# First part in a fixed order, its biases added later, and half of a layer's rows written by an adding DMA

## The chip, the cores and the metric

The kernel runs on one core of a Trainium2 chip. The metric is the time of one execution on the device in microseconds (us). Three executions of the kernel before took 2216.36, 2218.04 and 2220.47 us.

## The reference

A batch of one, 512 latent rows and 256 context rows of width 1024, passes two blocks of two layers each, all in fp32. The change lies in the first block:

```
for i in range(DEPTH):                                  # 2 layers
    sh1, sc1, g1, sh2, sc2, g2 = adaln(c, w_mod[i], b_mod[i])        # silu(c) @ w_mod + b_mod
    a_lat = modulate(x, norm1_g[i], sh1, sc1)           # rmsnorm(x, g) * (1 + sc) + sh
    # layer 0: pool mixer for x and ctx; layer 1: attention over ctx and x
    x = x + g1 * y_lat
    x = x + g2 * hier_moe(modulate(x, norm2_g[i], sh2, sc2), ...)
    # layer 0 does the same for the 256 context rows, with its own shift and scale

pool_mixer: four windows (2, 4, 8, 16), one to each 256 channels:
    y = (window mean of h - h) @ w_pool[g] + b_pool ;  return y * ls
hier_moe:  16 experts in 4 groups: the best group by g_logits, the best two experts in it,
    hid = silu(h @ w_gate) * (h @ w_up) * gates ;  sum of hid @ w_down
```

The second block (stick-breaking attention, dilated attention, two convolutional feed-forward parts) follows, and but for one small sum in the dilated attention it is left as it was.

## The kernel before

One program builds instructions for five engines: TensorE (PE), VectorE (DVE), ScalarE (ACT), GpSimd (POOL) and SyncE (SP). Each runs its own list in order; a scheduler sets the lists, mostly from the order in which the Python code emits the work and from when operands are expected. SP issues the weight loads (`load_raw`, L314) in pieces of 128 x 1024 fp32, 512 KB each, into 6 small buffers and a `ring` of larger ones; a load waits until its buffer is free and until its DMA semaphore, one of eight that all queues of SP and ACT share, has come free.

**First part (0 to 137 us).** x and ctx lie transposed, channels on partitions, in 8 chunks (`NCH`). The modulation is computed in blocks of 512 columns: `adaln_mm` (L380) multiplies by 16 matmuls and copies the result (L385, ACT); `adaln_end` transposes it (L177) and reduces it on DVE (L393). `pool_pre` makes normalized and shifted rows (L479, L481), `pool_win` runs a window over them (L495, L507), `pool_back` first adds the bias of the pool to x (L518, ACT), multiplies by the window's weight (L521) and adds the product to x (L523, DVE). `moe_chunk` scales a chunk (L587) and squares it (L589) on ACT and feeds both to the router's logits in a group of four matmuls (L594). `moe_close` evacuates the logits of one segment (L622), transposes and reduces them (L627), makes the reciprocal root mean square (`rstd_from`, whose root is L192) and leaves in `st.trs` one pair of functions to each block of 128 rows; `moe_tr` transposes such a block, and DVE writes it with scale and shift (L648) for a DMA to `h2d` in device memory (L649).

**The experts.** `moe_run` computes the routing on DVE (L685 to L780) with counting matmuls on PE between (L716 to L722, L775); the last result is the list of row indices per expert (L778). GpSimd gathers each expert's rows from h2d by index (L834); PE transposes them (L177), ACT and DVE split them in two fp32r parts (L854, L855), and weights are split likewise: ACT rounds `hi` (L294), DVE subtracts for `lo` (L295). Gate and up take three matmuls to each product (L353 to L355), down the same; ACT evacuates down's result (L898) and sends it off (L899). Layer 0 takes 768 rows with room for 128 per expert, layer 1 takes 512 with room for 96. `Stream.side("a")` and `side("b")` run two adaLN blocks of layer 1 just before layer 0's experts, and each of their halves lets one item more of the weights go (`st.more(1)`).

In the trace, tiles of 128 x 2048 are named s, tiles of 128 x 516 t, small ones sm, g and tv.

Of the kernel before, what the change touches and what calls it, by code (L numbers as in the profile page):

```python
# [25 lines left out]
D = 1024  # L26
NCH = 8
# [36 lines left out]
def build(tc, A, out, stop=None, dbg=None):  # L64
# [98 lines left out]
    def vc(name, i=0, n=1):  # L163
        o = _VEC[name] + i
        return vec[:, o : o + n]

# [155 lines left out]
    class Stream:  # L322
# [50 lines left out]
    def adaln_mm(l, nb, st=None, got=None):  # L373
# [3 lines left out]
        for u in range(2):  # L377
# [4 lines left out]
            if st:  # L382
                st.more(1)
# [128 lines left out]
    def pool_back(r, g):  # L512
        xr, n, _ = rows[r]
        ps_p = pooled.pop((r, g))
        g_, b_ = gl[r, g // 2]
        for f in range(2):
            c = 2 * g + f
            S.activation(xr[:, c, :], xr[:, c, :], AF.Identity, bias=b_[:, c % 4 : c % 4 + 1])  # L518
# [4 lines left out]
            V.scalar_tensor_tensor(xr[:, c, :], ps[:, :n], g_[:, c % 4 : c % 4 + 1], xr[:, c, :], op0=ALU.mult, op1=ALU.add)  # L523
# [29 lines left out]
    def moe_start(l, segs, cap):  # L553
# [5 lines left out]
        for xr, n, r in segs:  # L559
            q = K()  # L560
            q.xr, q.n, q.r, q.nb, q.tb0, q.psl, q.seen, q.due = xr, n, r, n // 128, st.ntb, None, 0, []
# [17 lines left out]
    def moe_chunk(st, i, c):  # L579
# [3 lines left out]
        if q.psl is None:  # L583
            q.psl = PS()
            q.hts = [s8() for _ in range(NCH * q.n // 2048)]
            q.a2 = gain_mod(st.l, "norm2_g", 4, q.r, f"a2_{q.r}")
        S.activation(hch(q, c), q.xr[:, c, :], AF.Copy, scale=q.a2[:, c : c + 1])  # L587
        sq = t2()
        S.activation(sq[:, : q.n], q.xr[:, c, :], AF.Square)  # L589
# [8 lines left out]
    def moe_shift(st, i):  # L598
# [11 lines left out]
        q.b2r = half("b2")  # L610
        for h_ in range(2):
            pt = PS()
            for c in range(4):
                transpose(pt[:, c * 128 : c * 128 + 128], b2[:, 4 * h_ + c : 4 * h_ + c + 1].to_broadcast([128, 128]))
            S.copy(q.b2r[:, 512 * h_ : 512 * h_ + 512], pt)

    def moe_close(st, i):
# [4 lines left out]
        S.copy(ev[:, :n], q.psl[:, :n])  # L622
# [5 lines left out]
        q.rs = rstd_from(lg[:, :, 20], 1.0 / D, [128, nb], f"n2_{q.r}")  # L628
        lg = lg[:, :, 0:20]
# [3 lines left out]
        def tr(b):  # L633
# [10 lines left out]
            def second():  # L644
                ht = half("ht")
                for h_, pt in enumerate(pts):
                    hs_ = slice(512 * h_, 512 * h_ + 512)
                    V.scalar_tensor_tensor(ht[:, hs_], pt, q.rs[:, b : b + 1], q.b2r[:, hs_], op0=ALU.mult, op1=ALU.add)  # L648
                (G if len(st.segs) > 1 else S).dma_start(st.h2d[(q.tb0 + b) * 128 : (q.tb0 + b) * 128 + 128, :], ht)  # L649
# [3 lines left out]
        st.trs += [tr(b) for b in range(nb)]  # L653

# [13 lines left out]
    def moe_run(st, wst):  # L668
# [121 lines left out]

        def late():


            gd = gsm([128, N, 4], tag="gd")
            V.tensor_tensor(gd, gl_, bc(gm.rearrange("p (n o) -> p n o", o=1), [128, N, 4]), op=ALU.subtract)
# [4 lines left out]
            v1, v2 = (gsm([128, N], tag=f"v{j}") for j in range(2))  # L800
            for v_, va in ((v1, v1a), (v2, v2a)):
                V.tensor_tensor(va, va, goh, op=ALU.mult)
                V.reduce_sum(v_, va, axis=AX.X)
            ed = gsm([128, N], tag="ed")
            V.tensor_tensor(ed, v2, v1, op=ALU.subtract)
# [34 lines left out]
        def gather(e):  # L840
            xg[e] = half("xg")
            gather_rows(xg[e][0:cap, :], idx[0:cap, e : e + 1])
# [16 lines left out]
        def gate_up(e):  # L859
# [10 lines left out]
            S.activation(sg[0:cap, 0:256], pg[0:cap, 0:256], AF.Silu)  # L870
            V.tensor_tensor(sg[0:cap, 256:512], sg[0:cap, 0:256], pg[0:cap, 256:512], op=ALU.mult)
            pgs[e] = sg

# [80 lines left out]
        for e in range(3):  # L954
            gather(e)
        wst.side("c")
        if not wgu:
            with tc.issue_after(gated.ins):
                moe_weights(st, wst, 0, V)
        rows_t(0)  # L960
        for e in range(NEXP + 1):
# [17 lines left out]
            if e == NEXP - 1:  # L979
                onehots(segs[0])  # L980
            if e < NEXP:
# [101 lines left out]


    mst = moe_start(0, rows, 128)
    sss = [stats(0)]
    adaln_block(0, 0)
    rb[0] = bcast(sss[0].compact("n1_0"), T)
    adaln_block(0, 2)
# [1429 lines left out]
```

## Time and profile before

| | |
|---|---|
| median of three executions | 2218.04 us (2216.36 to 2220.47) |
| the profiled execution | 2218.79 us, its span 2217.0 us |
| mean granted TensorE clock | 0.973 |
| PE, DVE, ACT, POOL busy | 93%, 64%, 50%, 23% of the span |

A busy share is the sum of an engine's instruction times over the span. The places of the change lie in the first 305 us and, for layer 1, in 600 to 706 us. A row of the timeline gives the start, the time, the engine and the line of neighbouring instructions of one form (xN of them), and in brackets how long the engine stood idle ahead of it and what released it.

### The profile page before, as it was taken

Reading aid. Unit: us, or ns where it says so; the run is one execution under the profiler, and the core shown is the slowest. Engines: PE = TensorE matmul, PEld = TensorE weight load, DVE = VectorE, ACT = ScalarE, POOL = GpSimd, SP = SyncE. Lnnn points to the kernel's source line nnn. Section 1 sums busy time; section 2 is a strip of 40 time slices with the busy share of each in tenths; the row PEclk is TensorE's granted clock in tenths of the full one; section 3 lists DMA queues with packets and bytes.
Section 4 is the critical chain, followed back from the end, with each engine's and each line's share of the span. In section 5 each row is a group of like instructions: output and inputs, shape, how many; then the busy total and the mean of one; then the engine's idle time right before and its main releaser. Section 6 shows DMA issues by size and latency. Waiting matters only on the chain.

```text
span 2217.0 us, 32294 instructions
## 1 busy us (share of the span) xinstructions
PE 2067.5 (93%) x12233; PEld 1683.7 (76%) x12233; DVE 1418.8 (64%) x2304; ACT 1102.1 (50%) x1967; POOL 509.6 (23%) x513
## 2 busy tenths in 40 slices
PE   6869998999994999999999999999999999999997
PEld 1348767788863767776698888999878888888997
DVE  4579878778726987367847666626363568565633
ACT  3648864488833886344434434324253455343422
POOL 1011021477201212245423101014100024101011
PEclk9889999999997999999999999999999999999998
DMA  9699973124606996321113333332322212333321
GB/s 376 260 351 398 417 282 101 50 77 137 217 21 219 369 391 211 99 77 48 58 52 102 94 100 91 98 93 68 97 86 86 67 48 89 101 96 96 96 77 39
DMA packets 94207, 323.43 MB, mean 146 GB/s; under 512 B 11537, under 2 KB 17184, under 8 KB 93536
## 3 DMA queue, kind: packets, MB, share of 16 engines
q1 hardware_dynamic: 76480, 274.76, 36.0%
q0 software_dynamic: 7968, 28.32, 3.6%
q10 hardware_dynamic: 9600, 18.26, 2.2%
q8 instruction: 97, 1.59, 0.3%
q14 instruction: 62, 0.51, 0.1%
HBM read 301.02 MB, written 20.27 MB: 145 GB/s over the span
## 4 chain that ended last, share of the span: by engine, by line
PE 65%; DVE 7%; DMA 4%; POOL 3%; ACT 3%; issue 3%; ACTq 0%; DVEq 0%; POOLq 0%; SPq 0%
PE ps L353 19%; PE ps L355 18%; PE ps L354 18%; PE ps L177 3%; DMA s<-in_mgu_dram 1%; PE ps L1722 1%; DVE lo L295 1%; POOL raw L1762 1%; PE ps L2103 1%; PE ps L2254 1%; DVE s L1939 1%; ACT hi L294 1%; DMA raw<-in_mdn_dram 1%; PE ps L2059 1%; DVE s L1931 1%
## 5 line engine op out<-in xcount | busy, mean ns | idle before, releaser
L353 PE MATMUL ps<-s,hi 128*128 128x512 f32 (+1 forms) x1440 | 513.5, 358 | 4.3 <-DVE s L1931 3.2
L354 PE MATMUL ps<-s,hi 128*128 128x512 f32 (+1 forms) x1440 | 505.6, 351 | 3.0 <-DVE s L1939 1.8
L355 PE MATMUL ps<-s,lo 128*128 128x512 f32 (+1 forms) x1440 | 507.4, 353 | 0.0
L294 ACT CAST hi<-raw 128x1024 fp32r<-128x1024 f32 x284 | 294.0, 1047 | 419.2 <-PE ps L354 334.2
L295 DVE TENSOR_TENSOR lo<-raw,hi 128x1024 fp32r<-128x1024 f32 x232 | 288.2, 1256 | 277.5 <-ACT hi L294 277.3
L295 POOL TENSOR_TENSOR lo<-raw,hi 128x1024 fp32r<-128x1024 f32 x52 | 125.4, 2411 | 892.1 <-ACT hi L294 892.1
L353 PEld LDWEIGHTS ps<-s,hi 128*128 128x128 f32 x1440 | 270.5, 188 | 45.7 <-issue 8.0
L354 PEld LDWEIGHTS ps<-s,hi 128*128 128x128 f32 x1440 | 271.3, 188 | 41.4 <-DVE s L1939 2.4
L355 PEld LDWEIGHTS ps<-s,lo 128*128 128x128 f32 x1440 | 271.1, 188 | 41.1 <-issue 0.5
L353 PE MATMUL ps<-hi,s 128*128 128x512 f32 (+1 forms) x528 | 216.8, 412 | 4.6 <-ACT hi L294 2.0
L354 PE MATMUL ps<-lo,s 128*128 128x512 f32 (+1 forms) x528 | 211.9, 401 | 2.6 <-DVE lo L295 2.6
L355 PE MATMUL ps<-hi,s 128*128 128x512 f32 (+1 forms) x528 | 211.3, 401 | 2.5 <-DVE s L1839 2.5
L355 PE MATMUL ps<-t2r,lo 128*128 128x256 f32 (+1 forms) x640 | 188.2, 294 | 0.0
L354 PE MATMUL ps<-t2r,hi 128*128 128x256 f32 (+1 forms) x640 | 187.8, 293 | 0.0
L353 PE MATMUL ps<-t2r,hi 128*128 128x256 f32 (+1 forms) x640 | 187.8, 293 | 0.0
L353 PEld LDWEIGHTS ps<-hi,s 128*128 128x128 f32 (+1 forms) x528 | 105.3, 199 | 30.1 <-ACT hi L294 4.4
L355 PEld LDWEIGHTS ps<-hi,s 128*128 128x128 f32 (+1 forms) x528 | 105.2, 199 | 29.0 <-DVE s L1839 4.1
L354 PEld LDWEIGHTS ps<-lo,s 128*128 128x128 f32 (+1 forms) x528 | 105.9, 201 | 25.7 <-DVE lo L295 3.1
L353 PEld LDWEIGHTS ps<-t2r,hi 128*128 128x128 f32 x640 | 121.2, 189 | 5.2 <-issue 2.5
L354 PEld LDWEIGHTS ps<-t2r,hi 128*128 128x128 f32 x640 | 121.1, 189 | 5.3 <-issue 2.5
L355 PEld LDWEIGHTS ps<-t2r,lo 128*128 128x128 f32 x640 | 120.8, 189 | 5.2 <-issue 2.5
L295 DVE TENSOR_TENSOR lo<-s,hi 128x1024 fp32r<-128x1024 f32 x98 | 114.8, 1217 | 5.2 <-ACT hi L294 4.7
(371 smaller groups left out, 3667.2 us busy)
## 6 DMA issues: line engine op xcount, KB each, us to landing
raw<-in_up_dram SPq DMA_DIRECT2D x88, 512.0 KB
s<-in_mgu_dram SPq DMA_DIRECT2D x64, 512.0 KB
raw<-in_mgu_dram SPq DMA_DIRECT2D x44, 512.0 KB
raw<-in_down_dram SPq DMA_DIRECT2D x44, 512.0 KB
raw<-in_dilqkv_dram SPq DMA_DIRECT2D x36, 512.0 KB
s<-in_mdn_dram SPq DMA_DIRECT2D x34, 512.0 KB
raw<-in_wmodT_dram SPq DMA_DIRECT2D x32, 512.0 KB
s<-in_wmod_dram SPq DMA_DIRECT2D x30, 512.0 KB
```

The lines of the kernel that those rows point to most:

```text
L177: return PE.transpose(dst, src, ident if idt is None else idt)
L294: S.copy(hi, raw)
L295: eng.tensor_tensor(lo, raw, hi, op=ALU.subtract)
L353: mm(ps, ahi, bhi, start=start, stop=False)
L354: mm(ps, ahi, blo, start=False, stop=False)
L355: return mm(ps, alo, bhi, start=False, stop=stop)
L1722: mm(po_[c][o : o + 64, qb * 128 : qb * 128 + 128], vview[:, kc, c // 2 * 64 : c // 2 * 64 + 64], PTs[h_][:, kc * 128 : kc * 128 + 128], s ...
L1762: G.tensor_tensor(w, w, crow, op=ALU.mult)
L1931: V.tensor_tensor(mv, mv, bc(self.rb[:, None, 0:256], [128, 2, 256]), op=ALU.mult)
L1939: V.scalar_tensor_tensor(self.h.lo(c)[:, ts], x[:, c, ts], g_, self.h.hi(c)[:, ts], op0=ALU.mult, op1=ALU.subtract)
L2059: mm(pz[:, o : o + n], qq, kk, start=True, stop=True)
L2103: mm(po[64 * hh : 64 * hh + 64, kb * 128 : 512], vt, at[:, o : o + n], start=(kb == 0), stop=(kb == 3), tile_position=(0, 64 * hh))
```

## The change

1. `in_order()` ties each instruction of DVE, ACT and PE in the first part to the one emitted before it on its engine. The first part is written anew: blocks of adaLN come in the order 0, 2, 1, 3, 4, 8, 5, 9, 6, 7, then 10 and 11 behind the fixed part, each loaded four blocks ahead; `pool_back` is split in `back_mm` and `back_add`; chunks of x go to the logits two by two as soon as they are done. The sums of squares of ctx go over ACT and PE (`sum_stats`).
2. The pool's bias is not added there. `moe_chunk` adds it inside its two activations, and x and ctx get it in the loop of layer 0's experts, one chunk of each in expert 4 to 11 (`back_bias`, called as `side`).
3. In layer 0 the first gather is issued ahead of nine small operations of `late` (now `late_first`); `side("a")` and `side("b")` let no weights go; the four items (eight loads) that they let go before are issued behind the first gather, and the first of them waits until it has landed.
4. In layer 1 the shift rows are made early and written to h2d for row blocks 0 and 1. Later ACT evacuates these blocks with their scale, and a GpSimd DMA adds them to what stands there. Blocks 2 and 3 are written as before, but from the queue of GpSimd. The load of the root's table comes right behind the copy of the logits. Five tiles join the weight ring before the output projection instead of behind it.
5. `norm_a` sums two values with a reduction instead of an addition.

```diff
+    @contextlib.contextmanager
+    def in_order():
+        cur = nc.cur_bb.bb.instructions
...
+            if i.engine in prev:
+                tc.add_manual_dep(i, prev[i.engine].name, mybir.DependencyInfo(
+                    mybir.DependencyClass.NoSync, mybir.DependencyReason.DATA), reason="in order")
...
     def side(self, k):
             for b in self.ads.get(k, ()):
-                adaln_mm(*b, self)
+                adaln_mm(*b, self, more=k not in ("a", "b"))
...
-            if st:
+            if st and more:
                 st.more(1)
...
-    def pool_back(r, g):
...
-            S.activation(xr[:, c, :], xr[:, c, :], AF.Identity, bias=b_[:, c % 4 : c % 4 + 1])
...
+    def back_bias(c):
+        for r, (xr, n, _) in enumerate(rows):
+            S.activation(xr[:, c, :], xr[:, c, :], AF.Identity, bias=gl[r, c // 4][1][:, c % 4 : c % 4 + 1])
+
+    def sum_stats(r):
...
+            S.activation(q[:, :n], xr[:, c, :], AF.Square)
+            for b in range(n // 128):
+                mm(ps[:, b : b + 1], q[:, b * 128 : b * 128 + 128], ones, start=(c == 0 and b == 0),
+                   stop=(c == NCH - 1 and b == n // 128 - 1))
...
+    def moe_chunk(st, i, c, bias=None):
...
+            S.activation(hch(q, c), q.xr[:, c, :], AF.Identity, scale=q.a2[:, c : c + 1], bias=q.a2b[:, c : c + 1])
+            S.activation(sq[:, : q.n], q.xr[:, c, :], AF.Square, bias=bias[c // 4][:, c % 4 : c % 4 + 1])
...
     def moe_close(st, i):
-        S.copy(ev[:, :n], q.psl[:, :n])
+        evac = S.copy(ev[:, :n], q.psl[:, :n])
+        if len(st.segs) == 1:
+            sqrt_table(evac)
...
-                ht = half("ht")
+                ht = wide() if len(st.segs) > 1 else half("ht")
...
+                    if b in q.there:
+                        st.s_last = S.activation(ht[:, hs_], pt, AF.Copy, scale=q.rs[:, b : b + 1])
+                    else:
+                        V.scalar_tensor_tensor(ht[:, hs_], pt, q.rs[:, b : b + 1], q.b2r[:, hs_], op0=ALU.mult, op1=ALU.add)
-                (G if len(st.segs) > 1 else S).dma_start(st.h2d[(q.tb0 + b) * 128 : (q.tb0 + b) * 128 + 128, :], ht)
+                if b in q.there:
+                    G.dma_start(to, ht, accum_op=ALU.add)
+                else:
+                    G.dma_start(to, ht)
...
+    def moe_shift_rows(st, i, there=()):
...
+            for b in there:
+                S.dma_start(st.h2d[(q.tb0 + b) * 128 : (q.tb0 + b) * 128 + 128, :], q.b2r)
...
-        for e in range(3):
+        first = gather(0)
+        with tc.issue_after(gated.ins):
+            firsts = late_first()
+        if wst.ads:
+            hold[:] = [first]
+            wst.more(2 * sum(len(v) for v in wst.ads.values()))
+        for e in range(1, 3):
             gather(e)
...
+            if e >= 4:
+                with tc.issue_after(silu[0].ins):
+                    side(e - 4)
...
-    pool_back(1, 3)
-    for c in range(4):
-        moe_chunk(mst, 1, c)
-    moe_tr(mst, 4)
-    for c in range(4, 8):
-        moe_chunk(mst, 1, c)
-    adaln_block(0, 10)
-    moe_close(mst, 1)
-    adaln_block(0, 11)
+    with in_order():
...
+        ad_mm(8, 7)
+        back_mm(0, 3)
+        ad_end(8)
+        chunks(0, 0)
+        pool_win(1, 0)
+        ad_mm(5, 10)
...
+        moe_close(mst, 0)
+        chunks(1, 1)
+        moe_tr(mst, 1)
...
+        moe_close(mst, 1)
+        moe_shift_rows(mst, 1)
+    for nb in (10, 11):
+        ad_mm(nb)
+        ad_end(nb)
...
-        V.tensor_tensor(rd, den[:, :, :, 0], den[:, :, :, 1], op=ALU.add)
+        V.reduce_sum(rd, den, axis=AX.X)
...
+    moe_shift_rows(mst, 0, there=(0, 1))
+    ring.extend(s8() for _ in range(5))
```

How the lists of the engines stand before and after is shown at three places. The first is the end of the first part on PE, before (t_976, t_1016 and t_1111 are the copies of adaLN blocks 10, 11 and (1,0), cs their operand, s_864 and s_805 the rows of ctx, tri that of the counting):

```order
L380 MATMUL ps_961<-rawx,cs 32x512 x4
L177 MATMUL ps_978<-ident,t_976 128x128 x4
L177 MATMUL ps_987<-ident,t_985 128x128 x2
L380 MATMUL ps_1003<-s_118,cs 32x512 x4
L380 MATMUL ps_1003<-s_119,cs 32x512 x4
L177 MATMUL ps_1018<-ident,t_1016 128x128 x4
L177 MATMUL ps_1078<-ident,s_864 128x128 x4
...
L380 MATMUL ps_1098<-s_121,cs 32x512 x4
L177 MATMUL ps_1113<-ident,t_1111 128x128 x4
L716 LDWEIGHTS tri
```

And after (mod_108 is the shift, whose rows are made here; t_959 the context's logits):

```order
L193 MATMUL ps_961<-ident,t_959 128x128 x2
L193 MATMUL ps_977<-ident,mod_108 128x128 x4
L396 MATMUL ps_989<-rawx,cs 32x512 x4
L193 MATMUL ps_1000<-ident,t_998 128x128 x4
L396 MATMUL ps_1007<-s_118,cs 32x512 x4
L193 MATMUL ps_1018<-ident,t_1016 128x128 x4
L193 MATMUL ps_1078<-ident,s_805 128x128 x4
...
L396 MATMUL ps_1098<-s_121,cs 32x512 x4
L193 MATMUL ps_1109<-ident,t_1107 128x128 x4
L787 LDWEIGHTS tri
```

The transposes of the context's logits have moved ahead of both blocks; what stands between block 10 and the counting is the same.

The second place is the opening of layer 0's experts in the list of SP, before, with the semaphores that a row waits on:

```order
L314 DMA s_118<-in_mgu_dram 128x1024 [waits DMAHW5_49,PE_49]
L314 DMA s_119<-in_mdn_dram 128x1024 [waits DMAHW6_49,PE_49]
L314 DMA s_119<-in_mdn_dram 128x1024 [waits DMAHW7_49,PE_49]
L314 DMA s_120<-in_mgu_dram 128x1024 [waits DMAHW0_49,PE_49]
L314 DMA s_120<-in_mgu_dram 128x1024 [waits DMAHW1_49,PE_49]
```

And after (DMASW are the semaphores of GpSimd's DMAs, g_1548 a count that the routing leaves):

```order
L330 DMA s_118<-in_mgu_dram 128x1024 [waits DMAHW5_49,PE_49]
L1078 TENSOR_LOAD g_1548 [waits DVE_49]
L1078 ISA x2
L330 DMA s_119<-in_mdn_dram 128x1024 [waits DMAHW6_49,DMASW6_49,PE_49]
L330 DMA s_119<-in_mdn_dram 128x1024 [waits DMAHW7_49,PE_49]
L330 DMA s_120<-in_mgu_dram 128x1024 [waits DMAHW0_49,PE_49]
L330 DMA s_120<-in_mgu_dram 128x1024 [waits DMAHW1_49,PE_49]
```

The loads from s_119 on stand behind the reading of a count and behind the first gather.

The third place is the opening of layer 1's experts on ACT, before:

```order
L622 COPY t_7000<-ps_6877 128x512 [waits PE_49]
L294 CAST hi_7183<-s_6973 128x1024 [waits DMAHW5_49]
L294 CAST hi_7187<-s_6973 128x1024 [waits DMAHW6_49,Pool_49]
L192 ACT_TABLE_LOAD
L192 ACTIVATE sm_7008<-g_6618,epst 128x4 [waits DVE_49]
L649 DMA h2d_6613<-s_7030 128x1024 [waits DVE_49] x2
```

After, on ACT:

```order
L668 COPY t_7017<-ps_6899 128x512 [waits PE_49]
L224 ACT_TABLE_LOAD
L224 ACTIVATE sm_7019<-epst 128x1
L208 ACTIVATE sm_7027<-g_6635,epst 128x4 [waits DVE_49]
L699 ACTIVATE s_7049<-ps_7039,sm_7035 128x512 [waits DVE_49,PE_49]
L699 ACTIVATE s_7049<-ps_7044,sm_7035 128x512 [waits PE_49]
...
L310 CAST hi_7202<-s_6662 128x1024 [waits DMAHW5_49]
```

And after, on POOL, where the four writes now stand ahead of the gather:

```order
L703 DMA h2d_6630<-s_7049 128x1024 [waits DMAHW2_49,Activation_49]
L703 DMA h2d_6630<-s_7049 128x1024 [waits DMAHW4_49,Activation_49]
L705 DMA h2d_6630<-s_7130 128x1024 [waits DVE_49] x2
L909 DMA s_7189<-h2d_6630,g_7179 96x1024 [waits DMASW6_49,DMASW5_49,DMASW7_49,DMASW4_49,DVE_49]
```

The casts of ACT have gone behind the root and four evictions, and the gather waits for four DMAs of its own queue instead of four of ACT's.

## Rows read from the trace of the kernel before

**Rows 1.** The page's part 4: the chain that ended last, share of the span.
```profile
PE 65%; DVE 7%; DMA 4%; POOL 3%; ACT 3%; issue 3%; ACTq 0%; DVEq 0%; POOLq 0%; SPq 0%
```

**Rows 2.** Windows; columns are length, PE, PEld, DVE, ACT, POOL busy, clock, DMA, GB/s.
```profile
50.00:100.00 50.00, 40.62 (x176) 14.83 (x172) 28.33 (x68) 27.37 (x58) 2.63 (x9) 0.89 0.84 322
100.00:150.00 50.00, 31.52 (x253) 22.31 (x254) 32.13 (x103) 17.25 (x34) 9.04 (x10) 0.77 0.75 292
...
130.00:140.00 10.00, 1.45 (x16) 0.96 (x16) 8.59 (x19) 0.04 (x1) 2.61 (x2) 0.65 1.03 418
160.00:170.00 10.00, 10.00 (x50) 8.21 (x49) 9.24 (x11) 8.87 (x13) 0.00 (x0) 1.00 0.77 234
200.00:230.00 30.00, 30.00 (x146) 24.63 (x146) 27.80 (x32) 26.32 (x37) 2.24 (x2) 1.00 1.03 417
...
750.00:800.00 50.00, 49.23 (x250) 35.21 (x250) 45.35 (x54) 43.26 (x65) 13.11 (x6) 1.00 1.03 382
```

**Rows 3.** Waits of SP's queue in 0 to 150: total, times, longest.
```profile
SPq L314 <- PE ps L380: 48.3, 12, 19.8
```

**Rows 4.** Line L518 in 0 to 150, by form: minimum, median, maximum in ns.
```profile
L518 ACT ACTIVATE x<-x,sm x8: 705/708/722, 48.2 to 65.5; 128x512 f32<-128x512 f32 x8
L518 ACT ACTIVATE xc<-xc,sm x8: 492/496/498, 67.8 to 97.6; 128x256 f32<-128x256 f32 x8
```

**Rows 5.** Timeline of DVE, POOL and PE, opening of layer 0's experts.
```profile
136.62 0.19 DVE L778 CAST g<-ps 128x28 int32<-128x28 f32 x1 [0.49 <-PE ps L775]
...
136.80 4.62 DVE L295 TENSOR_TENSOR lo<-raw,hi 128x1024 fp32r<-128x1024 f32 x4
...
137.09 1.82 POOL L834 DMA_INDIRECT s<-h2d,g  x1 [10.35 <-DVE g L780]
...
141.43 0.94 POOL L834 DMA_INDIRECT s<-h2d,g  x1 [0.30 <-issue]
...
145.39 1.94 PE L177 MATMUL ps<-ident,s 128*128 128x128 f32 x8 [8.81 <-DMA s<-h2d,g]
```

**Rows 6.** Timeline of ACT, two evictions of down in layer 0's loop.
```profile
194.81 1.07 ACT L898 COPY s<-ps 128x512 f32<-128x512 f32 x2
...
204.30 1.07 ACT L898 COPY s<-ps 128x512 f32<-128x512 f32 x2
```

**Rows 7.** Waits of SP's queue in 600 to 720: total, times, longest.
```profile
SPq L314 <- DMA h2d<-s: 55.2, 4, 48.8
```

**Rows 8.** Timeline of SP, ahead of layer 1's experts.
```profile
607.03 73.68 SPq L314 DMA_DIRECT2D raw<-in_mgu_dram  x4
```

**Rows 9.** Timeline of ACT, DVE, POOL and PE, opening of layer 1's experts.
```profile
670.91 0.58 ACT L622 COPY t<-ps 128x512 f32<-128x512 f32 x1 [0.20 <-PE ps L594]
...
672.24 0.51 DVE L627 TENSOR_REDUCE g<-ps 128x84 f32<-128x336 f32 x1 [3.74 <-PE ps L177]
...
673.40 1.28 ACT L192 ACT_TABLE_LOAD   x1
674.70 0.30 ACT L192 ACTIVATE sm<-g,epst 128x4 f32<-128x4 f32 x1
...
676.88 2.06 DVE L648 SCALAR_TENSOR_TENSOR s<-ps,sm,s 128x512 f32<-128x512 f32 x3
...
677.66 5.12 ACTq L649 DMA_DIRECT2D h2d<-s  x4
...
691.02 0.18 DVE L778 CAST g<-ps 128x26 int32<-128x26 f32 x1 [0.41 <-PE ps L775]
...
691.48 1.78 POOL L834 DMA_INDIRECT s<-h2d,g  x1 [53.51 <-DVE g L780]
...
698.84 1.51 PE L177 MATMUL ps<-ident,s 96*128 96x96 f32 x8 [7.85 <-DMA s<-h2d,g]
704.23 1.51 PE L177 MATMUL ps<-ident,s 96*128 96x96 f32 x8 [3.88 <-DMA s<-h2d,g]
705.45 0.72 PE L353 MATMUL ps<-hi,s 128*96 128x512 f32 x1
```

More of the change, by code (lines that the diff above doesn't have):

```diff
@@ L165, in vc @@
         return vec[:, o : o + n]
+    @contextlib.contextmanager
+    def in_order():
+        cur = nc.cur_bb.bb.instructions
+        n0 = len(cur)
+        known = {id(i) for i in cur}
+        yield
+        prev = {}
+        for i in cur:
+            if id(i) in known or i.engine not in (V.engine, S.engine, PE.engine):
+                continue
+            if i.engine in prev:
+                tc.add_manual_dep(i, prev[i.engine].name, mybir.DependencyInfo(
+                    mybir.DependencyClass.NoSync, mybir.DependencyReason.DATA), reason="in order")
+            prev[i.engine] = i
     def dump(name, ap):
@@ L789, in by_block, with late_first @@
             V.tensor_tensor(o, bc(col[:, :, None], o.shape), bc(ebase[128][0 : o.shape[0], None, 0:N], o.shape), op=ALU.subtract)
+        gd = gsm([128, N, 4], tag="gd")
+        ed = gsm([128, N], tag="ed")
+        def late_first():
+            V.tensor_tensor(gd, gl_, bc(gm.rearrange("p (n o) -> p n o", o=1), [128, N, 4]), op=ALU.subtract)
+            v1, v2 = (gsm([128, N], tag=f"v{j}") for j in range(2))
+            for v_, va in ((v1, v1a), (v2, v2a)):
+                V.tensor_tensor(va, va, goh, op=ALU.mult)
+                V.reduce_sum(v_, va, axis=AX.X)
+            return V.tensor_tensor(ed, v2, v1, op=ALU.subtract)
         def late():
-            gd = gsm([128, N, 4], tag="gd")
-            V.tensor_tensor(gd, gl_, bc(gm.rearrange("p (n o) -> p n o", o=1), [128, N, 4]), op=ALU.subtract)
             s_gd = S.activation(gd, gd, AF.Exp)
@@ L1146, in build, with ad_load, ad_mm, ad_end @@
-    moe_close(mst, 0)
-    pool_back(1, 3)
-    for c in range(4):
-        moe_chunk(mst, 1, c)
-    moe_tr(mst, 4)
-    for c in range(4, 8):
-        moe_chunk(mst, 1, c)
-    adaln_block(0, 10)
-    moe_close(mst, 1)
-    adaln_block(0, 11)
+    got = {}
+    def ad_load(nb):
+        got[nb] = adaln_load(0, nb)
+    def ad_mm(nb, nxt=None):
+        adaln_mm(0, nb, got=got.pop(nb))
+        if nxt is not None:
+            ad_load(nxt)
+    def ad_end(nb):
+        adaln_end(0, nb)
+    def chunks(i, j):
+        for c in (2 * j, 2 * j + 1):
+            moe_chunk(mst, i, c, bias=[gl[i, h_][1] for h_ in range(2) if (i, h_) in gl])
@@ L1839, in split_x @@
         V.scalar_tensor_tensor(h.lo(c), x[:, c, :], gains(i, j, c), h.hi(c), op0=ALU.mult, op1=ALU.subtract)
-    ring.extend(s8() for _ in range(5))
     wst = Stream(1, {})
```

209 lines of the change are left out of this document (123 added, 86 removed).

## The prediction

> **What bounds the kernel now.** I read the chain that ended last first: TensorE holds 65% of it, DMA 4%, VectorE 7%, GpSimd and ScalarE 3% each [rows 1]. So a gain must come from stretches in which TensorE stands still. The windows show where these are [rows 2]: it is busy 40.62 us of 50 to 100, 31.52 of 100 to 150, but all 30.00 us of 200 to 230, inside layer 0's experts, where the DMA share is 1.03 at 417 GB/s and ScalarE is busy 26.32. In layer 1's experts (750 to 800) it is busy 49.23. The change touches three places: the first part, the opening and loop of layer 0's experts, and the opening of layer 1's. I price each by what starts TensorE there.
>
> **First part: taken as nothing.** The new order is fixed on three engines, so a waiting instruction now holds everything behind it. The count of rows per expert (L716, now L787) stands in both orders right behind the transposes of block (1,0) (first pair of order listings), with the four row blocks' transposes and adaLN blocks 10 and 11 ahead of it. The biases that go (eight of 0.49 us for the context, eight more for x) leave ScalarE [rows 4], which is not what TensorE waits for here. What a better order could win at most is TensorE's idle time: 50 - 40.62 = 9.4 us before 100, and about 4.5 us in 100 to 130 (of the 18.5 us idle in 100 to 150, 8.55 lie in 130 to 140 and some 5.4 between 140 and 145.39, behind the index chain [rows 2, 5]), 13.9 in all. Against it, every block's copy on ScalarE and transposes on TensorE now stand behind whole groups of chunk and pooling work in a fixed row; I followed the new order with the rows' durations, and the router started some 3 us sooner, while the last blocks on TensorE, behind which L787 stands, were where they had been. I take 0 for the moment of the indices, 136.62 now, from -7 (half of the idle time won) to +4.
>
> **Layer 0, opening.** Before, the indices were done at 136.62, the first gather was issued at 137.09, and TensorE began on its rows at 145.39, after waiting 8.81 us for that DMA [rows 5]. Between them stood a full queue: share 1.03, 418 GB/s in 130 to 140 [rows 2]. After, eight loads of 512 KB wait for the first gather (second pair of listings: the load of `mdn` waits on a DMA that GpSimd issued). With little ahead of it the gather lands sooner: at the least nothing is won, at the most 8.81 us less the issue of 0.94 [rows 5] and a bare landing, some 5. I take -2.5, the middle. The nine small operations of late_first come ahead of the splits, but the splits (4.62 us for four) end before the rows are there in either case.
>
> The price stands behind it. Eight loads of 0.524 MB are 4.19 MB, which at the 418 GB/s of [rows 2] is 10.0 us of all DMA engines, left empty before the gather lands. What the loop could give back is what it left idle: in 160 to 170 the share was 0.77 instead of 1.03, 2.5 us. The other 7.5 us come out of the lead that the weights have on TensorE. If the lead is enough the price is 0, if the loop runs hard against DMA it is 7.5. I take +2, nearer to nothing, since TensorE had no idle time at all in 200 to 230, so the weights were not late there.
>
> **Layer 0, the biases in the loop.** The period of an expert is 204.30 - 194.81 = 9.49 us by the eviction copies [rows 6]. ScalarE is busy 26.32/30 of that, 8.33 us. From expert 4 to 11 each gets one bias on 512 and one on 256 columns: 0.71 (the 512-column bias in [rows 4]) + 0.49, and issued back to back a little less, some 1.1. That makes 9.4 of 9.49: just full. Cover is ScalarE's idle time, 1.16 us an expert; with the cover gone it would be 8 x 1.2 = 9.6 us in all. I take +1.
>
> Layer 0 then sums to 0 - 2.5 + 2 + 1 = +0.5.
>
> **Layer 1, opening.** Here the times are plainer. (a) Before, the copy of the logits ended at 671.49, the reduction at 672.75, but the square root began only at 674.70, since two weight casts and a table load of 1.28 stood ahead of it on ScalarE [rows 9]. After (third pair of listings), load and a small square root come right behind the copy: 671.49 + 1.28 + 0.30 = 673.1, and the casts behind. That is -1.6, at most -1.95. (b) Half of the eight evictions leave VectorE for ScalarE, 4 x 2.06/3 = -2.75; VectorE ran without a gap there, and all its router operations stood among them. So the indices come at 691.02 - 4.35 = 686.7. Late_first then delays the splits, not the gather. (c) TensorE began the first rows at 698.84, the second at 704.23, and the experts at 705.45, 1.22 behind. The gather of 691.48 took 1.78 to issue and over 5 us to land. The queue was busy because SyncE had been held: four loads took from 607.03 to 680.71, and SyncE's waits name the write of h2d as what held it, 48.8 us at the longest [rows 7, 8]; the weights behind it came down with the gathers. A semaphore that those loads share with ScalarE's h2d writes does that. After, these writes stand in GpSimd's queue, SyncE is free, and the weights are down before 686. If the landing stays as slow, only the 4.35 us are won; if the two gathers land in 2 us, the experts start at 686.7 + 0.46 + 2 x 0.94 + 0.30 + 2 + 1.22 = 692.5, 12.9 sooner. I take -9, near the middle. TensorE is nearly full from there on, so this goes to the end.
>
> (d) What is added: two early copies of b2 rows into h2d, while DMA is slack, and two accumulating DMAs. No row shows one. Below, one costs no more than a plain write; above, the ScalarE queue's four writes, 5.12 us to issue, had landed by 691.48, 8.7 us after, without holding the gather. The accumulating two can be issued from about 677.5 on, the last plain write about 681. To 686.7 that is 9 and 5.5 us of cover. I take 0. In the sum of pairs in norm_a the work only changes its form; nothing.
>
> A price beside (a): the table load took 1.28 us, and the root began 1.30 behind its start [rows 9]. The Trainium skill (ScalarE: Activation LUTs, What ACT_TABLE_LOAD costs) adds a drain of 1.38 us to it. By that, moving the load would give 1.4 us more and the sum would be -9.9; the trace shows no such drain, so I stay by the row.
>
> **Sum:** +0.5 - 9 = -8.5 us. The profiled execution took 2218.79 (span 2217.0 and 1.8 around it), so 2210.3; the median lies 0.75 lower, which makes 2209.5. I say **2210**.
>
> **Rivals.** *The debt of the held loads* (0.21). The loop of layer 0 keeps share 1.03 from start to end, with no room to catch up, and ScalarE is full. All 7.5 us are felt instead of 2, and some of the biases: layer 0 +7 or so, in all 2217. For it: DMA and TensorE are both full in 200 to 230. Against it: 0.77 in 160 to 170 shows a lead.
>
> *The fixed order holds a late block* (0.09, the other side). SyncE waited 48.3 us, 19.8 at the longest, for TensorE to be done with adaLN weights before it could load on [rows 3]. With loads four blocks ahead and no engine allowed past a block that is late, each such wait stops pooling and logits too. 14 us, less than the longest one, gives 2224; from 9 us on it decides.
>
> *The accumulating write is late* (0.07). Above 9 us from issue, or if a POOL-queue write needs more than 5.5, the gather of layer 1 waits and its gain falls to some 3: 2216. The gathers beside VectorE's splits took 1.78 and 1.82 to issue, alone 0.94 [rows 5, 9], so GpSimd's issues can double; four writes would then cost some 3.5 us more. The Trainium skill (SBUF — State Buffer, Who interferes with whom) says that GpSimd is locked out of a port while VectorE reads two SBUF inputs or runs a two-port mode, and that such DMAs seem stalled; the rows just named agree. The evictions beside which these writes are issued read PSUM, which speaks against it here.
>
> *The first part does get shorter* (0.12). Half of TensorE's idle time is won, 7 us: 2203.
>
> **How the numbers follow.** The forecast has 0.51, with its own range of 2204 to 2216. 0.2% is 4.4 us, about what can be told from no change here: faster is below 2213.6, slower above 2222.4. Faster: nine tenths of the forecast's 0.51, the 0.12, and a little of the debt and of the late write, 0.62. Slower: the 0.09, and the upper end of the debt with the biases on the path, 0.14. The rest, 0.24, lies between. The range 2200 to 2221 leaves out the late block, and half of the shorter first part.
>
> **What would show it.** In layer 1: a table load directly behind the copy of the logits, indices near 686.7, no long wait of SyncE after 607, the experts' first product at 694 to 699. In layer 0: indices within 4 us of 136.6, the first gather's wait under 7 us, ScalarE near full in 200 to 260, and the last product of the loop within 3 us of where it was. I am wrong if TensorE shows gaps behind weights in 150 to 300, if the gather of layer 1 waits for h2d, or if the first part moved by more than 5 us.

## The result and the profile after

The changed kernel takes 2244.7 us (median of 4 executions, 2242.76 to 2246.13), the kernel before 2218.45 on the same chip (4 executions): a ratio of 1.0118, interval 1.01 to 1.0135. The forecast was 2210. The profiled execution has a span of 2241.0 us, 24.0 more than before.

Six moments cut each profiled execution into stretches: the indices of layer 0 done; its first gate product; the last product of its loop; the first product of the projections behind it (qkv); the reduction of layer 1's logits; layer 1's first gate product. Lengths in us, from the start of one row of the timeline to the start of the next; e18 and the others are experiments, told below.

| | to indices | to first product | loop | to qkv | attention | layer 1, to product | rest | span |
|---|---|---|---|---|---|---|---|---|
| before | 136.62 | 12.86 | 154.94 | 32.87 | 334.95 | 33.21 | 1511.55 | 2217.0 |
| after | 146.01 | 9.35 | 166.19 | 34.87 | 340.54 | 31.04 | 1513.00 | 2241.0 |
| after, once more (e5) | 143.00 | 9.15 | 168.38 | 34.06 | 334.15 | 26.34 | 1509.72 | 2224.8 |
| layer 1 alone (e3) | 136.42 | 12.91 | 156.25 | 34.11 | 336.19 | 30.77 | 1513.45 | 2220.1 |
| no ties (e9) | 133.11 | 9.04 | 166.56 | 34.87 | 337.32 | 31.22 | 1512.38 | 2224.5 |
| yd write on GpSimd (e17) | 142.17 | 8.92 | 156.20 | 35.56 | 343.21 | 28.88 | 1512.56 | 2227.5 |
| e13 | 129.16 | 12.12 | 162.90 | 34.97 | 338.80 | 26.28 | 1514.37 | 2218.6 |
| e18 | 129.25 | 12.18 | 153.91 | 33.64 | 337.16 | 25.63 | 1514.73 | 2206.5 |

So of the 24.0 us, +9.4 came up in the first part, -3.5 at the first gather, +11.3 in the loop, +2.0 behind it, +5.6 in the attention, -2.2 in layer 1 and +1.5 in the rest.

The windows of the changed kernel, to set beside [rows 2] (same columns), and two of the kernel before:

```profile
100.00:130.00 30.00, 21.59 (x139) 12.20 (x140) 16.24 (x62) 13.47 (x28) 2.37 (x4) 0.89 0.31 117
130.00:140.00 10.00, 6.58 (x72) 3.12 (x69) 4.31 (x13) 4.19 (x6) 1.06 (x2) 0.98 0.73 283
140.00:150.00 10.00, 0.94 (x13) 0.54 (x12) 9.18 (x28) 1.00 (x3) 2.91 (x3) 0.50 0.15 48
...
200.00:230.00 30.00, 29.56 (x141) 23.45 (x141) 27.71 (x31) 28.96 (x44) 3.60 (x4) 1.00 1.03 416
270.00:280.00 10.00, 3.65 (x20) 2.76 (x18) 1.32 (x2) 1.56 (x3) 0.00 (x0) 0.81 1.02 414
280.00:290.00 10.00, 6.82 (x22) 5.17 (x23) 7.30 (x9) 7.68 (x10) 0.00 (x0) 0.68 1.03 417
```

Before:

```profile
100.00:130.00 30.00, 26.02 (x220) 17.67 (x220) 19.68 (x70) 14.03 (x28) 3.44 (x6) 0.90 0.57 208
270.00:280.00 10.00, 10.00 (x50) 8.24 (x49) 9.97 (x12) 9.54 (x14) 0.00 (x0) 1.00 1.03 420
```

Two places are new. From 100 to 130 the DMA share is 0.31, where it was 0.57: few weights come while no engine is full. And from 270 to 290, near the end of layer 0's loop, TensorE is busy 10.47 of 20 us while DMA is full; before, it had no idle time there. ScalarE is busier in 200 to 230 by 28.96 - 26.32 = 2.6 us, some 0.8 an expert, which fits the biases.

**First part.** SyncE's longest wait for TensorE (total, times, longest), in 0 to 150, after:

```profile
SPq L330 <- PE ps L396: 57.5, 13, 29.7
```

In [rows 3] it was 19.8. In the timeline at the end of the first part, L310 and L311 are the splits of the weights (L294 and L295 before), L401 and L409 the copy and the reduction of an adaLN block, L849 the indices and L909 the gather:

```profile
137.74 1.04 ACT L310 CAST hi<-raw 128x1024 fp32r<-128x1024 f32 x1 [4.17 <-DMA h2d<-pw]
138.69 0.58 ACT L401 COPY t<-ps 128x512 f32<-128x512 f32 x1
...
139.32 0.83 PE L193 MATMUL ps<-ident,t 128*128 128x128 f32 x4 [2.63 <-ACT t L401]
140.19 0.19 DVE L409 TENSOR_REDUCE mod<-ps 128x8 f32<-128x32 f32 x1 [3.86 <-PE ps L193]
...
146.01 0.19 DVE L849 CAST g<-ps 128x28 int32<-128x28 f32 x1 [0.49 <-PE ps L846]
...
146.48 1.02 POOL L909 DMA_INDIRECT s<-h2d,g  x1 [13.13 <-DVE g L870]
...
150.99 1.94 PE L193 MATMUL ps<-ident,s 128*128 128x128 f32 x8 [5.02 <-DMA s<-h2d,g]
```

VectorE stands 3.86 us behind the transposes of the last adaLN block, which stand behind ScalarE's copy, which stands behind a weight cast that waits for a write to h2d. All index work of VectorE is queued behind it. The gather itself did what was forecast: issued 0.47 us behind the indices, 1.02 to issue, and TensorE waits 5.02 us instead of 8.81 [rows 5].

**Loop.** ScalarE, the queues of SyncE and ScalarE, VectorE and TensorE at the gap (L975 evicts down's result, L976 sends it off, L929 and L930 split an expert's rows):

```profile
270.09 1.08 ACT L975 COPY s<-ps 128x512 f32<-128x512 f32 x2 [0.72 <-DMA yd<-s]
...
279.63 2.46 SPq L330 DMA_DIRECT2D raw<-in_mgu_dram  x2
280.49 0.33 ACTq L976 DMA_DIRECT2D yd<-s  x1
280.86 0.58 ACT L929 CAST s<-ps 128x512 fp32r<-128x512 f32 x1 [9.20 <-DMA s<-in_mdn_dram]
...
281.47 0.69 DVE L930 TENSOR_TENSOR s<-ps,s 128x512 fp32r<-128x512 f32 x1 [9.10 <-ACT s L929]
...
282.71 0.79 PE L369 MATMUL ps<-hi,s 128*128 128x512 f32 x1 [9.06 <-ACT hi L310]
```

The eviction of down was done at 271.2, but its write to `yd` was issued only at 280.49. Behind it in ScalarE's list stands the cast L929, and its 9.20 us of idle time are put down to the DMA of a weight piece, which the cast does not read. VectorE and TensorE wait 9.1 us for ScalarE.

**Attention.** In `norm_a` (VectorE), beside GpSimd's products for the next modulation:

```profile
523.40 18.87 POOL L1886 TENSOR_TENSOR raw<-raw,xc 128x1024 f32<-128x1024 f32 x8
542.16 0.55 POOL L1735 CAST s<-s 128x384 fp32r<-128x384 f32 x1
542.62 1.05 POOL L1736 TENSOR_TENSOR s<-ktok,s 128x384 fp32r<-128x384 f32 x1
543.58 6.98 POOL L1886 TENSOR_TENSOR raw<-raw,xc 128x1024 f32<-128x1024 f32 x3
```

VectorE's copies of the same form:

```profile
518.86 0.43 DVE L1857 COPY t<-sm 128x512 f32<-128x512 f32 x1
...
540.54 10.30 DVE L1857 COPY t<-sm 128x512 f32<-128x512 f32 x1
```

The same copy takes 0.43 us at 518.86, when GpSimd is idle, and 10.30 at 540.54; it ends 0.3 us behind the last of these products of GpSimd (543.58 + 6.98 = 550.56). TensorE's longest wait there is 8.7 us, for the VectorE work behind the copy.

**Layer 1.** The opening of the experts, to set beside [rows 9]:

```profile
695.63 0.58 ACT L668 COPY t<-ps 128x512 f32<-128x512 f32 x1 [1.14 <-PE ps L646]
696.23 1.28 ACT L224 ACT_TABLE_LOAD   x1
...
696.96 0.51 DVE L675 TENSOR_REDUCE g<-ps 128x84 f32<-128x336 f32 x1 [3.74 <-PE ps L193]
697.63 0.28 ACT L208 ACTIVATE sm<-g,epst 128x4 f32<-128x4 f32 x1
...
700.47 2.04 POOL L703 DMA_DIRECT2D h2d<-s  x2 [37.85 <-ACT s L699]
...
711.56 0.18 DVE L849 CAST g<-ps 128x26 int32<-128x26 f32 x1 [0.40 <-PE ps L846]
...
713.66 1.46 SPq L330 DMA_DIRECT2D s<-in_mdn_dram  x2
714.10 1.52 POOL L909 DMA_INDIRECT s<-h2d,g  x1 [10.29 <-DVE lo L311]
715.92 1.93 POOL L909 DMA_INDIRECT s<-h2d,g  x1 [0.30 <-issue]
...
722.60 1.51 PE L193 MATMUL ps<-ident,s 96*128 96x96 f32 x8 [11.08 <-DMA s<-h2d,g]
```

From the reduction to the indices it is 14.60 us; before it was 691.02 - 672.24 = 18.78. But the gather is issued 2.54 us behind the indices instead of 0.46, and 0.44 us behind the next loads of SyncE (713.66); its rows come later still. Windows of 2 us show the writes to h2d (same columns):

```profile
702.00:704.00 2.00, 0.00 (x0) 0.00 (x0) 1.93 (x11) 2.00 (x3) 1.62 (x3) 0.72 1.08 152
704.00:706.00 2.00, 0.49 (x11) 0.40 (x11) 1.39 (x7) 1.98 (x3) 0.00 (x0) 0.50 1.12 188
706.00:708.00 2.00, 0.00 (x0) 0.00 (x0) 1.73 (x9) 0.38 (x1) 0.00 (x0) 0.50 0.96 188
708.00:710.00 2.00, 0.00 (x0) 0.00 (x0) 1.90 (x9) 0.00 (x0) 0.00 (x0) 0.50 1.02 399
710.00:712.00 2.00, 0.61 (x8) 0.39 (x8) 1.60 (x8) 0.07 (x1) 0.00 (x0) 0.50 0.28 111
```

All DMA engines are busy from 702 to 710, but for the first 6 us at 152 to 188 GB/s, and then at 399. The first 6 us moved 1.06 MB, which is two writes of 0.524 MB, and two adding writes stand in the queue ahead of two plain ones: the slow stretch fits the adding ones.

### The profile page after: what moved, and what is told of

Same layout as the page of the kernel before. It is cut to its first block, busy times and chain, and to the rows that moved or that the text cites. A ratio compares the mean times of both kernels' runs of the same rounds, so it can differ in the third digit from the quotient of the medians.

```text
span 2241.0 us, 32342 instructions
## 1 busy us (share of the span) xinstructions
PE 2077.6 (93%) x12257; PEld 1690.6 (75%) x12257; DVE 1424.3 (64%) x2303; ACT 1108.6 (49%) x1972; POOL 508.0 (23%) x514
## 4 chain that ended last, share of the span: by engine, by line
PE 64%; DVE 8%; DMA 4%; POOL 3%; issue 2%; ACT 2%; DVEq 0%; ACTq 0%; POOLq 0%; SPq 0%
PE ps L369 18%; PE ps L371 18%; PE ps L370 18%; PE ps L193 3%; DMA s<-in_mgu_dram 2%; PE ps L1846 1%; DVE lo L311 1%; POOL raw L1886 1%; PE ps L2228 1%; PE ps L2379 1%; PE ps L2427 1%; DVE s L2064 1%; DVE t L1857 1%; PE ps L2184 1%; DVE s L2056 1%
## 5 line engine op out<-in xcount | busy, mean ns | idle before, releaser
L310 ACT CAST hi<-raw 128x1024 fp32r<-128x1024 f32 x282 | 291.8, 1047 | 413.4 <-PE ps L370 331.8
L311 DVE TENSOR_TENSOR lo<-raw,hi 128x1024 fp32r<-128x1024 f32 x231 | 287.4, 1257 | 276.1 <-ACT hi L310 275.6
L311 POOL TENSOR_TENSOR lo<-raw,hi 128x1024 fp32r<-128x1024 f32 x51 | 122.9, 2409 | 871.5 <-ACT hi L310 871.5
L311 DVE TENSOR_TENSOR lo<-s,hi 128x1024 fp32r<-128x1024 f32 x99 | 116.2, 1217 | 9.8 <-ACT hi L310 8.9
```

Of the source, the lines that this page charges most:

```text
L310: S.copy(hi, raw)
L311: eng.tensor_tensor(lo, raw, hi, op=ALU.subtract)
```

## The experiments

Ratios are to the kernel before on the same chip, with 95% intervals. The changed kernel's executions differ more than those of before: e5 is the same kernel again.

**The changed kernel again (e5).** No edit.

> The changed kernel once more, so that the following three stand beside it on one chip: 1.010 to 1.012 times the kernel before.

Ratio 1.0079 (1.0053 to 1.0105), less than expected, executions from 2226.51 to 2245.38. The profiled one was the shortest: the copy in `norm_a` took 2.39 us there, and the gather of layer 1 was issued 0.46 us behind the indices. First part and loop were about as long as in the first trace (143.00 and 168.38): these two stay, the other two depend on the execution.

**One edit put back or made alone (e1, e2, e3, e4).**

```diff
 e1, on after:  -V.reduce_sum(rd, den, axis=AX.X)
                +V.tensor_tensor(rd, den[:, :, :, 0], den[:, :, :, 1], op=ALU.add)
 e2, on before: the same line the other way round
 e3, on before: the whole of part 4 of the change, and nothing else of it
 e4, on after:  part 4 taken out
```

> The changed kernel with only the small sum of norm_a put back as an addition of two operands. Theory (the 10.30 us copy on VectorE behind GpSimd's chain comes from the reduction, which does not take GpSimd's turn as the addition did): the copy falls to about 1.3 us, the time to about 2237, 7 to 8 us under the changed kernel. Rival (the copy meets GpSimd's chain only because the attention now starts at another moment): 2244, with a long copy or addition still there.

> The kernel before with only the small sum of norm_a as a reduction. Theory: about +7, 2225, with one copy of some 10 us in 520 to 535. Rival (chance of the moment): no difference from 2218. Forecast on record: 0 for this edit.

> The kernel before with only the opening of layer 1's experts changed (shift rows early and written ahead, two blocks added by DMA, table load early, all four writes from GpSimd's queue, ring extended early). Theory from the trace of the changed kernel: indices 4.2 us sooner, 2 us of it lost again since the accumulating writes keep the DMA engines busy at 180 GB/s until about the time of the gather, in all about -2: 2216. Rival: the gain of 9 us forecast, 2209, where the weights come earlier than in the changed kernel.

> The changed kernel with the opening of layer 1's experts as before, apart from the order of the nine small operations. Theory: about 2 us slower than the changed kernel, 2246. Rival (the accumulating writes cost more than they save): equal or faster, 2240 to 2244.

e1: 1.0077 (1.0053 to 1.01). The stall did not go; it moved to the addition, which took 10.56 us. e2: 0.9987 (0.9974 to 1.0), copy 2.2 us. The form of the sum is not the cause. e3: 0.9971 (0.9955 to 0.9987), faster than before; first part and loop stay within 1.4 us of before. e4: 1.0081 (1.006 to 1.0101), the same as e5, with indices at 141.08 and a loop of 168.54: the loss of the first part and of the loop lies in parts 1 to 3.

**What the loop's gap needs (e6, e7).**

```diff
 e6: -adaln_mm(*b, self, more=k not in ("a", "b"))
     +adaln_mm(*b, self, more=True)
     -hold[:] = [first]
     -wst.more(2 * sum(len(v) for v in wst.ads.values()))
 e7: -fin, fetch = moe_run(mst, wst, lambda c: back_bias(c) if c < NCH else None)
     +fin, fetch = moe_run(mst, wst)
```

> The changed kernel, but the eight loads go before the gather again, two at a time beside the two adaLN blocks, as in the kernel before. Theory A (the 9.1 us gap of TensorE at 272 us is the debt of the ten us in which DMA stood empty): the gap goes, the first gather takes 3 us longer, in all 6 to 8 us faster than the changed kernel. Theory B (the gap comes from ScalarE, which is full with the biases and blocks at its send of an expert's result): the gap stays, 0 to 3 us slower.

> The changed kernel without the biases in the loop of layer 0's experts; the pool's bias is left out of x and ctx, all else is done. Theory A: within 2 us of the changed kernel, the gap at 272 us stays. Theory B: the gap goes, 8 to 10 us faster.

e6: 1.0072 (1.0049 to 1.0095), loop 156.71, but 12.00 us from the indices to the first product. e7: 1.0038 (1.0011 to 1.0065), loop 157.83. Either edit alone takes the gap away in its profile, so here it takes both parts to make it. In time e7 is 10.0 us below e5, as theory B had it, but e6 only 0.8, where theory A expected 6 to 8.

**The write that waits (e17).** One edit on the changed kernel, with hold, biases and ties kept:

```diff
-                S.dma_start(yd[e * cap : e * cap + cap, :], yt[0:cap, :])
+                (G if len(st.segs) > 1 else S).dma_start(yd[e * cap : e * cap + cap, :], yt[0:cap, :])
```

> The changed kernel with one edit: in layer 0 the write of an expert's result (yd) goes out on GpSimd's queue, not ScalarE's. If the gap of 9 us in layer 0's loop is ScalarE standing behind that write, whose DMA semaphore is taken by a weight load that is not down yet, the gap goes and the loop takes 156 to 158 us (166 to 168 before this edit). If the gap is the weights themselves, late by what the held loads left undone, TensorE waits for them all the same and the loop stays at 163 to 168. First part, attention and layer 1 as in the changed kernel.

Loop 156.20; ratio 1.002 (0.9998 to 1.0042). ScalarE goes straight from the eviction to the cast:

```profile
266.25 1.07 ACT L975 COPY s<-ps 128x512 f32<-128x512 f32 x2
267.21 1.08 ACT L929 CAST s<-ps 128x512 fp32r<-128x512 f32 x2
```

The weights were not late: with DMA at 1.03 in 250 to 270 as before the edit, TensorE's longest wait between 150 and 305 is 1.0 us. The gap was ScalarE standing behind its own write, as the first theory had it.

**What holds the first part (e8, e9, e14, e15).**

```diff
 e8:  -ht = wide() if len(st.segs) > 1 else half("ht")
      +ht = half("ht")
 e9:  -if i.engine in prev:                      # no ties at all
      +if False:
 e14: -i.engine not in (V.engine, S.engine, PE.engine)
      +i.engine not in (PE.engine,)              # ties on TensorE alone
 e15: +i.engine not in (S.engine,)               # ties on ScalarE alone
```

> The changed kernel with the rows for h2d in the small tiles of before instead of those that the weight splits use too. Theory: the weight cast of ScalarE that waited 4.17 us for a write to h2d does not wait, the copy of adaLN block (1,1) behind it comes 4 us sooner, the indices too, and it is 3 to 4 us faster than the changed kernel. Rival (the small tiles are too few, so that the evictions wait in their place): no difference.

> The changed kernel with the same code in the same sequence, but without the ties of in_order, so that the scheduler may move instructions past a waiting one. Theory (a waiting instruction holds all behind it): the indices come 3 to 6 us sooner than the 143 to 148 us of the changed kernel. Rival (the sequence itself and TensorE's clock set the end of the first part): indices within 2 us of the changed kernel.

> The changed kernel with its fixed order on TensorE alone; VectorE and ScalarE may be set by the scheduler. If what holds the first part is TensorE standing behind a late block in its row: indices at 142 to 146, as with all ties. If it is ScalarE's or VectorE's row: 132 to 136.

> The changed kernel with its fixed order on ScalarE alone. If ScalarE's row holds the first part (copies of a block behind the cast that waits 4.17 us for a write of h2d, or behind whole groups of chunk work): indices at 142 to 146. If it is TensorE's row: 132 to 136. If neither this nor the run with TensorE's ties comes to 142, it takes the ties on several engines together, or on VectorE.

e8: indices at 148.37, ratio 1.0081 (1.0054 to 1.0108): the wide tiles, though a wait on them stands in the trace, are not the cause. e9: indices at 133.11, 3.5 us sooner than before and sooner than expected; ratio 1.001 (0.9988 to 1.0032). Other profiles bear this out: the indices came at 129.2 to 133.3 in four without ties (e9, e13, e16, e18), at 135.1 to 138.4 in five with the first part of before, at 141.1 to 148.8 in nine with all ties. In e9 the DMA share in 100 to 130 is 0.57 again, and SyncE's longest wait for TensorE is short:

```profile
SPq L330 <- PE ps L396: 48.2, 14, 17.9
```

e14: indices at 131.56, ratio 1.0023 (1.0005 to 1.004); e15: 134.07 and 1.0026 (1.0011 to 1.0041). So neither TensorE's row nor ScalarE's holds the first part by itself. It takes ties on several engines, or VectorE's; these were not run apart.

**The copy on ScalarE (e10).**

```diff
-        V.tensor_copy(rdx..., bc(rd...))
+        S.copy(rdx..., bc(rd...))
```

> The changed kernel with the copy of 512 columns in norm_a on ScalarE instead of VectorE. Theory (VectorE's copy is held by GpSimd's multiplications that stand back to back): no instruction of VectorE takes 10 us in the attention, the stretch from the first product of the attention's projection to the reduction of layer 1's logits takes some 335 us instead of 341 to 345, the kernel is 6 to 8 us faster than the changed one. Rival (another operation of VectorE with two operands waits in its place): no difference.

On ScalarE the copy takes 0.63 to 0.64 us, beside the same products of GpSimd; TensorE's longest wait in 515 to 560 is 0.6 instead of 8.7, so the wait went as the theory had it. The size did not: the stretch took 338.47 instead of the expected 335, and the median is 3.3 us below e5, not 6 to 8; ratio 1.0046 (1.0027 to 1.0065).

**Adding or plain writes in layer 1 (e11, e12).** e3 with `there=()`, so that all four writes are plain, and with `there=(0,)`, one adding.

> The kernel before with layer 1's opening changed but for the adding: all four blocks are evicted by VectorE and written plainly from GpSimd's queue; table load and ring as in the change. Theory (the adding DMAs keep the DMA engines busy at some 180 GB/s until past the indices, which sends the gather behind the weights): indices 2.7 us later than with the adding, about 17.3 us after the reduction of the logits, but the gather follows at once, and the experts start 26 to 29 us after the reduction, against 30.8 with the adding and 33.2 before: 4 to 7 us faster than before. Rival (writes take as long plain): 32 us or more, no gain.

> As with two blocks added, but only one. Theory: the writes are down before the indices, these come 16 us after the reduction, the experts start 25 to 27 us after it, 6 to 8 us faster than before. Rival: one adding DMA is as late as two, 30 us.

e11: 0.9986 (0.9962 to 1.001), 16.98 us from the reduction to the indices, 31.05 to the first product. e12: 0.999 (0.9971 to 1.001), 15.66 and 29.44. With two adding writes (e3) it was 14.61 and 30.77. In e11 the four writes, issued from 676.98 on, ran at 330 to 354 GB/s (DMA share 0.80 to 0.87) and were down by 686, long before the indices at 690.08. In e3 the gather was issued 1.92 us behind the indices, in e11 0.97: adding won 2.4 us for the indices and lost 2.1 of them again up to the product. Neither run started the experts as soon as its theory had it (26 to 29 and 25 to 27): adding alone is not what keeps layer 1 from the forecast.

**All mended together (e13, e16, e18).** e13 is the changed kernel with the edits of e9, e6 and e10. e16 is e13 with `there=()`. e18 is e13 with the edit of e17.

> The changed kernel with three of its own parts taken out: no ties in the first part, no holding of loads behind the first gather (the two adaLN blocks let weights go again), and in the attention the copy behind the sum of pairs goes to ScalarE. If the three places are the causes and add up: indices near 133, 12 from there to the first gate product, the loop 156 to 157, the attention's part 333 to 338, in all 2208 to 2213 us profiled, ratio 0.995 to 0.999 (faster than before). If the places are tied to each other (what one gives is taken by the next, a loop that starts sooner meets its weights later), the loop is above 160 and the ratio at 1.000 or above.

> As the run with three parts taken out, and in layer 1 all four writes plain, none adding: ACT doesn't evacuate early, no b2 rows are written ahead. If the adding writes cost more than ScalarE's evictions save: from the reduction of layer 1's logits to the first gate product 45 to 47 us, as against 41 to 46 with adding writes, but without the late gathers; the time within 3 us of that run on either side. If adding pays: 3 us or more slower than it.

> The kernel with three parts taken out (no ties, no holding of loads, copy on ScalarE), and the yd write of layer 0 on GpSimd's queue as well. There the loop took 162.9 us with two waits of 2.4 and 0.9 us, and ended within 0.3 us of where the kernel before ended it. If the write on ScalarE's queue makes these waits: loop 156 to 158, 2211 to 2214 profiled, ratio 0.995 to 0.997. If the weights bound it (no more than 102.4 MB can be down sooner): loop 161 to 163 and the ratio as there, 0.998.

e13: 0.9979 (0.9967 to 0.9992). The ratio is as the first case had it, the loop of 162.90 as the second, and the profiled time of 2220.33 us is above the expected 2213: with the indices 7.5 us sooner than before, ScalarE stood 3.4 us behind its write again, and TensorE waited up to 2.4. e16: 0.9983 (0.9967 to 0.9998); 31.94 to layer 1's first product, as against 26.28 in e13, 5.7 us more in that profile, though the two medians differ by 2.1 us only; what adding is worth there is not settled. (The 45 to 47 and 41 to 46 us of the expectation are not this stretch, which took 25.6 to 33.2 in all profiles.) e18: 2212.19 us, ratio **0.9938** (0.9913 to 0.9963), loop 153.91: faster than both kernels, and beyond what was expected. In it the gather of layer 1 goes out 0.71 us behind the indices, the second one still ahead of SyncE's next loads, and the first rows are there 5 us behind the first issue:

```profile
680.75 0.18 DVE L849 CAST g<-ps 128x26 int32<-128x26 f32 x1 [0.40 <-PE ps L846]
681.46 0.97 POOL L909 DMA_INDIRECT s<-h2d,g  x1 [8.47 <-DVE g L871]
682.74 0.93 POOL L909 DMA_INDIRECT s<-h2d,g  x1 [0.30 <-issue]
682.86 1.50 SPq L330 DMA_DIRECT2D s<-in_mdn_dram  x2
...
686.44 1.51 PE L193 MATMUL ps<-ident,s 96*128 96x96 f32 x8 [5.73 <-DMA s<-h2d,g]
```

## Why the prediction was wrong, point by point

- **First part, taken as 0: wrong by 9.4 us, and the step that failed first.** The upper bound of 4 was set by following the new row with durations, as if each engine were held by its own work alone. (The idle time that it counts as about 4.5 us in 100 to 130 is 3.98 by the window of before.) The rival with a late block, given 0.09, had the right cause, the ties, and the right sign: without them (e9) the loss went and 3.5 us were won besides. The new code order is good; the ties cost 13 us (146.01 to 133.11; 10 against the 143.00 of e5). That what they hold is a late block fits SyncE's longest wait for TensorE, 29.7 us instead of 19.8, and the DMA share of 0.31; how several tied engines hold each other was not taken apart further.
- **Gather, -2.5: right in kind, -3.5.** e6, without the hold, gives 12.00 instead of some 9.
- **Loop, +2 for the debt and +1 for biases: +11.3, the largest miss, by a wait that has no term.** With the write out of the way (e17) the loop is 1.3 us longer than before, as long as in e3, so the two terms themselves were not too small. The forecast counted busy time, DMA bytes and ScalarE's cover of 1.16 us an expert. It did not ask what stands in ScalarE's list behind a DMA issue. The kernel before has the same wait, at the same line of the code:

```profile
266.14 0.33 ACTq L899 DMA_DIRECT2D yd<-s  x1
266.51 0.59 ACT L854 CAST s<-ps 128x512 fp32r<-128x512 f32 x1 [2.11 <-DMA s<-in_mgu_dram]
```

  There it held ScalarE 2.11 us, and TensorE did not feel it (its longest wait for ScalarE in that loop is 0.7). That the write waits because its DMA semaphore is one of eight shared with SyncE's weight loads fits the releaser named in both traces, a weight load, but was not tried; shown is that the wait belongs to that queue (e17). The rival of the debt (0.21) named the right place, but not the cause: the weights were there.
- **`norm_a`, nothing: wrong by 5.6 us in this execution,** and not by the edited line, as e1 and e2 show. The stall was in eight of the ten profiles with ties and the copy on VectorE (not in e5 and e15), and in none of e9, before, e2, e3, e11 and e12. With it the stretch took 340.5 to 345.5 us, without it 332.9 to 338.8. In e5 GpSimd ran just as densely and the copy got through in 2.39 us; what decides it stays open.
- **Layer 1, -9: the indices right, the landing of the gathers wrong, in all -2.2.** Indices -4.2 for a forecast of -4.35, by steps (a) and (b). The Trainium skill (ScalarE: Activation LUTs, What ACT_TABLE_LOAD costs) adds a drain of 1.38 us to the load. The root began 1.40 us behind the load's start with a small activation of 0.20 between, so this trace shows none either. From the indices to the first product the forecast had 14.4 us fall to 9.8; they rose to 16.44, and two steps failed there.
  - Step (c), the weights down ahead of the gathers. SyncE was freed of the long wait for h2d: 12.3 us at the longest instead of 48.8 [rows 7]. But it then stood 50.6 us for buffers that VectorE frees, and its next loads came 2.1 us behind the indices, among the gathers. From the first gather's issue to the product it took 13.90 us, as before (13.97).
  - Step (d), the adding writes at 0. The first was issued 11.1 us ahead of the indices, but they ran at about half of the plain rate of e11, and the four were down only at about the time of the indices; the gather was issued 2.1 us later than before. In e14 and e17, where it goes out 1.9 and 2.0 us behind the indices, its wait is put down to a write of h2d; here to VectorE's split, so for this profile the cause is likely, not shown. The rival of the late write named this step, at 0.07.

  All twenty profiles sort by one thing, which the forecast did not ask. SyncE's next loads come 2.1 us behind the indices with part 3 (its nine small operations delay VectorE's splits), 1.4 without. In six profiles the first two gathers are issued ahead of them (e4, e5, e7, e10, e13, e18), and the first product comes 11.0 to 12.5 us behind the indices; in the other fourteen the second is behind them, and it comes after 13.6 to 17.4, with plain writes (e11, e16) too. With the changed opening (all of the six but e4) this gives a stretch of 25.6 to 26.7 us, a gain of 6.5 to 7.6. No run moved these loads alone, so this order is seen, not shown, to be the cause.

## What to carry to other kernels

Before adding work to an engine that also issues DMAs, look in its queue for issues that already wait, and for what is queued behind them: a wait of 2 us that TensorE did not feel became 9 us on the path, and putting the issue on another queue removed it. Fixing an order on three engines at once cost 10 to 13 us here, where the same code left to the scheduler won 3.5, so try the new code order without ties first. Several changes that each look small meet in one buffer, queue or moment; run the parts alone and then together, since here one part alone (e3) was faster, all together were slower, and all with three causes mended and one write moved were the fastest.

## What the runs showed of the hardware

- **A VectorE copy of 0.43 us took 10.30 behind GpSimd,** from the middle of one GpSimd instruction to the end of the fifth behind it. The Trainium skill (SBUF — State Buffer, Who interferes with whom) says that a VectorE copy in a two-port mode and a GpSimd instruction lock each other out for a whole instruction. The trace agrees that there is blocking, though no run shows the copy's mode, and one GpSimd product is 18.87/8 = 2.36 us, and the copy was held across several; in e5 it got through beside the same products in 2.39. ScalarE's copy beside the same products took 0.63.
- **Adding DMAs of 512 KB moved at 152 to 188 GB/s** with a DMA share of about 1.0; the plain ones behind them reached 399, and four plain ones in e11 330 to 354 with a share of 0.80 to 0.87.
- **The same instructions end the first part at different times:** 146.01 and 143.00 us in two profiles of the changed kernel, and its executions spread over some 20 us. A difference of 3 us in one stretch between two single profiles is therefore no effect by itself.
